# The down projection of an encoder block as one level of Strassen, with the activations' combinations kept in DRAM

## The chip, the cores and the metric

The kernel runs on one core of one Trainium2 chip. The metric is the device time of one execution in microseconds (us); lower is better. Three runs of the kernel before took 2248.24, 2250.68 and 2250.88 us, so its median is 2250.68 us.

## The reference, cut to what matters

```python
D_MODEL = 2048; SEQ = 512
D_FF = 5632                       # 44 tiles of 128 features
x = x + jnp.concatenate([ya, yb], axis=-1) @ w_out[l]     # after two groups of attention heads
h = rmsnorm(x, norm_ffn[l])
x = x + (jax.nn.silu(h @ w_gate[l]) * (h @ w_up[l])) @ w_down[l]
return rmsnorm(x, norm_final)
```

Everything is float32. The change concerns the feed-forward part: gate and up (2048 to 5632 each), their gated product, and the down projection (5632 to 2048).

## The kernel before, in words

**Precision.** Each float32 operand is split into a rounded high part and the rest, a low part, both of type fp32r. A product is three matmuls, high x high, high x low and low x high (`mm3`, lines 187 to 190). So every weight tile is loaded by DMA (SP's queue), cast to its high part by ScalarE (`act.copy`) and subtracted to its low part by VectorE (`dve.tensor_sub`).

**Order.** TensorE's instructions keep the order in which the program writes them (line 49). Those of the other engines and the DMAs are placed by a scheduler: program order is their priority, and an instruction may come forward when its data and its buffer are there.

**Stages.** Input projection with attention; output projection (`unit_out`); gate/up (`unit_gu`, 44 units, one for each feature tile); down projection (`unit_dn`, then `unit_last`).

**Gate/up** already works as one level of Strassen (the Winograd form with seven products). The 2 x 2 blocks are: up and gate on one side, halves of a pair of model tiles on the other, and the two halves of the 512 positions. `turn_x` (line 523) makes, for each of the eight pairs of model tiles, the seven combinations of the normalized input, 128 x 7 x 512 (high and low), and they stay on chip in the tiles `cp0` to `cp5`, `w0` and `w1`. For each unit `load_gu` (line 569) loads four blocks of weights, 512 KB each, three into the ring of places m0 to m5 and one into a staging buffer `st`; `make_gu` (line 580) adds them up on VectorE and splits each of the seven operands into high and low. The products run in the order of line 563; `made_gu` (line 604) keeps three products ahead, in five pairs of buffers. Each product is 8 pairs x 3 = 24 matmuls of 256 columns, and a unit 168. Four PSUM banks take the seven products: `al` takes 11 and 12, `be` s2, `gm` s3 and 22, `de` s1 and s4 (line 615). Between products, `after` (line 630) adds them up. At the end of the unit VectorE and ScalarE make the gated product (lines 670 to 673), and its 128 x 512 tile goes to DRAM (`acts_kept`).

**Down.** `act_tile` (line 677) loads a tile from `acts_kept` and splits it; 28 such tiles stay on chip. `unit_dn` (line 697) runs twice (20 tiles each) over four groups of 512 output columns. For each it accumulates four banks, one for each 128 positions: 20 x 4 x 3 = 240 matmuls of 512 columns. The activations are the stationary operand, the weights move. `batch` and `fetch` (lines 114 to 136) load and split the weights, one batch of two tiles ahead. `to_rest` adds the scaled result to the residual, which `load_rest` has put on chip. `unit_last` does the last four feature tiles, position tile by position tile and group by group, with the final normalization (`finish`) behind each.

```python
    for p in range(2):
        for g in range(4):
            drive(unit_dn(p, g))
    load_gfin()
    drive(unit_last())
```

Of the kernel before, what the change touches and what calls it, by code (L numbers as in the profile page):

```python
# [17 lines left out]
P = 128  # L18
# [10 lines left out]
HC = (NCH - 1) // 2  # L29
NP = KT // 2  # L30
LAST_OUT = 4 * 8 + 2 * H * 6 - 1
# [13 lines left out]
def encoder_block(ctx: ExitStack, tc: tile.TileContext, io):  # L45
# [40 lines left out]
    def y_tile():  # L86
        return pools["ys"].tile([P, 512], F32, name="y")

    def c_tile():
        return pools["acts"].tile([P, 1024], F32R, name="ac")  # L90
# [15 lines left out]
    for p in range(2):  # L106
        for g in range(4):
            order += [io["w4"][c, g, b] for c in range(p * HC, (p + 1) * HC) for b in range(2)]
    order += [io["w4"][NCH - 1, g, b] for g in range(4) for b in range(2)]
# [4 lines left out]
    def fetch():  # L114
        i = len(ready)
        st = wst.tile([P, 1024], F32, name="st")
        if i >= len(order) - 8:
            hi, lo = c_tile(), c_tile()
# [11 lines left out]
    def batch():  # L130
        i = state["next"]
        state["next"] += 1
        last = LAST_OUT if i <= LAST_OUT else len(order) - 1
        while len(ready) <= min(i + (AHEAD if i else 0), last):
            fetch()
        return ready[i]
# [319 lines left out]
    def unit_out(c):  # L456
        xr = []
        b = [bank() for _ in range(NT)]
        for kb in range(8):
            wh, wl = batch()  # L460
            if c == 3 and kb == 4:
                load_gu(0)
            if c == 3 and kb == 7:
                for n in PRODUCTS[:2]:
                    make_gu(0, n)
# [22 lines left out]
        if c == 3:  # L488
            for n in PRODUCTS[2:4]:
                make_gu(0, n)  # L490
        for t in range(NT):
            y = y_tile()
# [69 lines left out]
    acts = {}  # L562
    PRODUCTS = ("11", "s2", "s3", "s1", "12", "22", "s4")
    OPERAND = {"11": 0, "12": 1, "s4": 2, "s1": 3, "s2": 4, "s3": 5, "22": 6}
    made, raws, ring = [], {}, [0]

    at = [0]

    def load_gu(f):
        w = {}  # L570
        for j, n in enumerate(("11", "22", "21", "12")):
            if n == "21":
                w[n] = wst.tile([P, 1024], F32, name="st")
            else:
                w[n] = place(at[0] % 6)
                at[0] += 1
            nc.sync.dma_start(w[n], io["w3"][f, j])
        raws[f] = w

    def make_gu(f, n):  # L580
        if n == "11":
            if f + 1 < NF:
                load_gu(f + 1)
        w = raws[f]
        if n == "s2":
            w["s3"] = wst.tile([P, 1024], F32, name="st")
            dve.tensor_add(w["s3"], w["11"], w["21"])
            w["s1"] = w["21"]
# [3 lines left out]
        elif n == "s4":  # L592
            w["s4"] = w["s2"]
            dve.tensor_add(w["s4"], w["s2"], w["12"])
        i = ring[0]
        ring[0] += 1
        j = i % 5
        hi = place(6 + j, F32R) if j < 2 else wsh.tile([P, 1024], F32R, name="hi")
        lo = place(8 + j, F32R) if j < 2 else wsl.tile([P, 1024], F32R, name="lo")
        act.copy(hi, w[n])  # L600
        dve.tensor_sub(lo, w[n], hi.bitcast(F32))  # L601
        made.append((hi, lo))

    def made_gu(f, i):
        while len(made) <= min(f * 7 + i + (3 if f or i else 0), NF * 7 - 1):
            make_gu(*divmod_gu(len(made)))
        return made[f * 7 + i]

    def divmod_gu(j):
        return j // 7, PRODUCTS[j % 7]  # L610

    def unit_gu(f):

        al, be, gm, de = bank(), bank(), bank(), bank()
        into = {"11": al, "s2": be, "s3": gm, "s1": de, "12": al, "22": gm, "s4": de}
        s = slice(0, 256)
        u2, g = w_tile(), w_tile()
        t = w_tile()

        def product(i, pairs):  # L620
            n = PRODUCTS[i]
            wh, wl = made_gu(f, i)
            o = into[n][:, s]
            for p in pairs:
                x = x1t[p][:, OPERAND[n]]
                ws = slice(p * P, (p + 1) * P)
                mm3(o, wh[:, ws], wl[:, ws], x[:, :256], x[:, 256:], start=p == 0 and i < 4,
                    stop=p == NP - 1, skip_group_check=True)

        def after(i):  # L630
            if i == 0:
                act.copy(u2[:, s], al[:, s])
            elif i == 1:
                dve.tensor_add(u2[:, s], be[:, s], u2[:, s])
            elif i == 2:
                dve.tensor_add(t[:, s], gm[:, s], u2[:, s])
            elif i == 3:
                dve.tensor_add(g[:, 256:], de[:, s], t[:, s])
            elif i == 5:
                dve.tensor_add(g[:, s], gm[:, s], u2[:, s])  # L640
            elif i == 6:
                dve.tensor_add(t[:, 256:], de[:, s], u2[:, s])

        if f == 0:
# [8 lines left out]
            for i in range(4):  # L653
                product(i, range(6, 8))
                after(i)
                yield
        else:
            for i in range(4):
                product(i, range(8))
                after(i)  # L660
                yield
        for i in range(4, 7):
            product(i, range(8))
            after(i)
            if f == NF - 1 and i == 4:
                for n in range(2):
                    act_tile(n)
                    fetch()
            yield
        dve.tensor_mul(g, g, pools["rb2"])  # L670
        act.activation(g, g, AF.Silu, scale=-1.0)
        dve.tensor_mul(g[:, s], al[:, s], g[:, s])
        dve.tensor_mul(g[:, 256:], g[:, 256:], t[:, 256:])
        nc.sync.dma_start(acts_kept[f], g)


    def act_tile(f):
        if f not in acts:
            src = y_tile()
            nc.sync.dma_start(src, acts_kept[f])  # L680
            a = pools["mk"].tile([P, 1024], F32R, name=("raw", "sums")[f]) if f < 2 else c_tile()
# [5 lines left out]
    def load_rest():  # L687
        for t in range(NT):
            for c in range(4):
                y = pools["rest"].tile([P, 512], F32, name=f"rest{t}{c}")  # L690
                nc.sync.dma_start(y, x1_kept[t, c])
                rest[t, c] = y
# [3 lines left out]

    def unit_dn(p, g):
        b = [bank() for _ in range(NT)]
        fs = range(p * HC * CF, (p + 1) * HC * CF)
        for f in fs:  # L700
            if f % 2 == 0:
                w = batch()
            if g == 0:
                act_tile(min(f + 1, fs[-1]))
            elif g == 3:
                act_tile(min(fs[-1] + 1 + (f - fs[0]) // 5, NF - 1))
            a = act_tile(f)
            ws = slice((f % 2) * 512, (f % 2 + 1) * 512)
            for t in range(NT):
                mm3(b[t], a[:, t * P:(t + 1) * P], a[:, 512 + t * P:512 + (t + 1) * P],  # L710
                    w[0][:, ws], w[1][:, ws], start=f == fs[0], stop=f == fs[-1])
            yield
        for t in range(NT):
            to_rest(t, g, b[t])

    def unit_last():
        w = [batch() for _ in range(8)]
        for t in range(NT):
            for g in range(4):
                b = bank()  # L720
                for f in range(CF):
                    a, (wh, wl) = act_tile((NCH - 1) * CF + f), w[g * 2 + f // 2]
# [3 lines left out]
                yield  # L726
                to_rest(t, g, b)
# [4 lines left out]
    def load_gfin():  # L732
        for j in range(2):
            t = c_tile().bitcast(F32)
# [79 lines left out]
    for n in ("mx", "xa"):  # L814
        pools[n].release()
    pools["acts"] = stage("acts", 28)
    pools["rest"] = stage("rest", 1, "right")
    load_rest()
    for p in range(2):
        for g in range(4):  # L820
            drive(unit_dn(p, g))
    load_gfin()
# [69 lines left out]
```

## Time and profile before

| | |
|---|---|
| median of three runs | 2250.68 us |
| profiled execution | 2248.8 us, span 2246.6 us |
| TensorE clock granted, mean | 0.997 |
| busy VectorE, ScalarE over the span | 64%, 39% |
| DMA, mean | 115 GB/s; HBM read 236.41 MB, written 19.92 MB |
| gate/up | about 879 to 1758 us of the span |
| down projection | about 1758 to 2236 us, of which `unit_last` about the last 43 |

How to read it: PE is TensorE, PEld its weight loads, DVE is VectorE, ACT is ScalarE, POOL is GpSimd, SP issues DMAs. The page of the profile gives each engine's busy time, the chain of work that ended last, and groups of instructions by line with the mean time of one. Matmuls overlap each other, so the mean of one matmul (283 ns for 256 columns) is not what it costs; the number of them in a stretch of 100 us says that. The table of windows gives, for each stretch: its length, then busy time and count of each engine, the clock granted to TensorE (1.00 is full), the busy share of the 16 DMA engines, and GB/s.

### The profile page before, as it was taken

Reading aid. Unit: us, or ns where it says so; the run is one execution under the profiler, and the core shown is the slowest. Engines: PE = TensorE matmul, PEld = TensorE weight load, DVE = VectorE, ACT = ScalarE, POOL = GpSimd, SP = SyncE. Lnnn points to the kernel's source line nnn. Section 1 sums busy time; section 2 is a strip of 40 time slices with the busy share of each in tenths; the row PEclk is TensorE's granted clock in tenths of the full one; section 3 lists DMA queues with packets and bytes.
Section 4 is the critical chain, followed back from the end, with each engine's and each line's share of the span. In section 5 each row is a group of like instructions: output and inputs, shape, how many; then the busy total and the mean of one; then the engine's idle time right before and its main releaser. Section 6 shows DMA issues by size and latency. Waiting matters only on the chain.

```text
span 2246.6 us, 34376 instructions
## 1 busy us (share of the span) xinstructions
PE 2229.2 (99%) x14386; PEld 2032.8 (90%) x14386; DVE 1432.2 (64%) x2066; ACT 879.6 (39%) x1229; POOL 0.2 (0%) x4
## 2 busy tenths in 40 slices
PE   9999999999999999999999999999999999999998
PEld 8888888888888888999999999999999888888886
DVE  5655555677686348878888788878887532422236
ACT  6333333454564344444444344443444421311223
POOL 0000000000000000000000000000000000000000
PEclk9999999999999999999999999999999999999999
DMA  8222222222223452444433443334442743433342
GB/s 300 84 77 77 82 76 76 76 75 75 75 66 105 149 187 89 128 132 132 120 111 119 118 127 119 111 120 118 127 117 90 252 138 101 137 94 100 98 150 75
DMA packets 82714, 258.54 MB, mean 115 GB/s; under 512 B 9568, under 2 KB 9952, under 8 KB 82560
## 3 DMA queue, kind: packets, MB, share of 16 engines
q1 hardware_dynamic: 80256, 252.17, 35.8%
q10 hardware_dynamic: 2304, 4.20, 0.5%
q8 instruction: 112, 1.84, 0.3%
q14 instruction: 42, 0.34, 0.0%
HBM read 236.41 MB, written 19.92 MB: 114 GB/s over the span
## 4 chain that ended last, share of the span: by engine, by line
PE 98%; DVE 1%; ACT 0%; DMA 0%; issue 0%; SPq 0%; ACTq 0%
PE bank L189 32%; PE bank L190 32%; PE bank L188 32%; PE bank L307 1%; PE bank L407 1%; PE bank L408 1%; PE bank L535 0%; PE bank L432 0%; DMA st<-w 0%; PE bank L184 0%; DVE lo L125 0%; DVE w L546 0%; DVE sm L409 0%; DVE at L414 0%; ACT at L410 0%
## 5 line engine op out<-in xcount | busy, mean ns | idle before, releaser
L125 DVE TENSOR_TENSOR lo<-st,hi 128x1024 fp32r<-128x1024 f32 (+1 forms) x209 | 254.5, 1218 | 404.6 <-ACT hi L124 400.9
L124 ACT CAST hi<-st 128x1024 fp32r<-128x1024 f32 (+1 forms) x209 | 218.9, 1047 | 488.8 <-PE bank L190 356.0
L189 PE MATMUL bank<-cp,hi 128*128 128x256 f32 x1104 | 312.8, 283 | 0.0
L190 PE MATMUL bank<-cp,lo 128*128 128x256 f32 x1104 | 312.2, 283 | 0.0
L188 PE MATMUL bank<-cp,hi 128*128 128x256 f32 x1104 | 310.2, 281 | 0.0
L189 PE MATMUL bank<-lo,ac 128*128 128x512 f32 x608 | 236.6, 389 | 0.0
L188 PE MATMUL bank<-hi,ac 128*128 128x512 f32 x608 | 236.6, 389 | 0.0
L190 PE MATMUL bank<-hi,ac 128*128 128x512 f32 x608 | 236.5, 389 | 0.0
L600 ACT CAST hi<-m 128x1024 fp32r<-128x1024 f32 x130 | 136.4, 1049 | 226.0 <-PE bank L189 153.3
L189 PE MATMUL bank<-cp,m 128*128 128x256 f32 x744 | 210.5, 283 | 0.0
L188 PEld LDWEIGHTS bank<-cp,hi 128*128 128x128 f32 x1104 | 210.3, 191 | 0.0
L190 PE MATMUL bank<-cp,m 128*128 128x256 f32 x744 | 210.2, 282 | 0.0
L188 PE MATMUL bank<-cp,m 128*128 128x256 f32 x744 | 208.7, 280 | 0.0
L189 PEld LDWEIGHTS bank<-cp,hi 128*128 128x128 f32 x1104 | 207.8, 188 | 0.0
L190 PEld LDWEIGHTS bank<-cp,lo 128*128 128x128 f32 x1104 | 207.7, 188 | 0.0
L188 PE MATMUL bank<-xt,hi 128*128 128x512 f32 x512 | 205.9, 402 | 0.0
L190 PE MATMUL bank<-xt,lo 128*128 128x512 f32 x512 | 200.6, 392 | 0.0
L189 PE MATMUL bank<-xt,hi 128*128 128x512 f32 x512 | 200.0, 391 | 0.0
L601 DVE TENSOR_TENSOR lo<-m,hi 128x1024 fp32r<-128x1024 f32 x130 | 159.0, 1223 | 51.5 <-ACT hi L600 50.1
L600 ACT CAST m<-m 128x1024 fp32r<-128x1024 f32 x90 | 94.4, 1049 | 152.1 <-PE bank L189 104.2
L189 PE MATMUL bank<-lo,xt 128*128 128x256 f32 x512 | 145.0, 283 | 0.5 <-DVE lo L125 0.5
L188 PE MATMUL bank<-hi,xt 128*128 128x256 f32 x512 | 144.9, 283 | 0.1
(216 smaller groups left out, 4965.4 us busy)
## 6 DMA issues: line engine op xcount, KB each, us to landing
st<-w SPq DMA_DIRECT2D x259, 512.0 KB, 3.5
m<-w SPq DMA_DIRECT2D x132, 512.0 KB, 4.1
acts_kept<-wk SPq DMA_DIRECT2D x44, 256.0 KB, 4.3
y<-acts_kept SPq DMA_DIRECT2D x44, 256.0 KB, 4.3
at<-x SPq DMA_DIRECT2D x8, 512.0 KB, 8.9
wk<-x SPq DMA_DIRECT2D x16, 256.0 KB, 5.4
x_kept<-y ACTq DMA_DIRECT2D x16, 256.0 KB, 4.5
rest<-x_kept SPq DMA_DIRECT2D x16, 256.0 KB, 5.4
```

The source lines that it names most:

```text
L124: act.copy(hi[:, s], st[:, s])
L125: dve.tensor_sub(lo[:, s], st[:, s], hi[:, s].bitcast(F32))
L188: pe.matmul(out, lh, rh, start=start, stop=False, **kw)
L189: pe.matmul(out, lh, rl, start=False, stop=False, **kw)
L190: pe.matmul(out, ll, rh, start=False, stop=stop, **kw)
L307: pe.transpose(b[:, j * P:(j + 1) * P], prob[:, j * P:(j + 1) * P], ident)
L407: pe.matmul(b, q[:, qs], kh[:, cs], start=True, stop=False)
L408: pe.matmul(b, q[:, qs], kl[:, cs], start=False, stop=True)
L600: act.copy(hi, w[n])
L601: dve.tensor_sub(lo, w[n], hi.bitcast(F32))
```

## The change

**Down.** Pair 0 of feature tiles is done in the old way by `unit_first` (four groups, 96 matmuls of 512 columns), the last two pairs by `unit_last` as before. The 19 pairs between go through `unit_dn(c, u)` in five chunks of pairs (4, 4, 4, 4, 3) and four groups u of 512 output columns. One such unit is a Strassen level with seven products: each is pairs x 2 tiles of positions x 3 matmuls of 256 columns, with the combinations of activations as the stationary operand. The weights come as four blocks of 256 columns for each pair (`w5`, 512 KB a block for four pairs) and pass through the same `make` as gate/up's, now with four pairs of buffers instead of five. The results are added on chip into `acc` tiles; after the last chunk `add_x1` loads the residual and adds it.

**Combinations.** After each second gate/up unit `keep_combos` makes the seven combinations of the pair's activations, splits them (four tiles through three buffers) and stores them in DRAM, 128 x 7 x 512 float32, 1.84 MB for a pair. `load_operands` loads them again through GpSimd's queue into seven slots, the tiles that held gate/up's operands: chunk 0 at the start of `unit_first`, later ones three pairs during the second unit of the chunk before and a fourth at the chunk's start, where the first four products run over the three early pairs first.

**Gate/up.** The order of the products is new, and except in the first unit one bank `al` takes 11, s2, s1 and s4 one on the other; running sums are copied out by ScalarE after the first three products. The load of the next unit's weights stands at product 12 instead of 11.

**The end.** The weights and activations of `unit_last` use slots of `xa` and the common buffers, and are prepared in the last down unit and in `unit_last` (`prepare_last`, `last_pair`), no longer spread over the second half of the down projection.

```diff
+CHUNKS = [range(1 + 4 * c, min(5 + 4 * c, 20)) for c in range(5)]
+DN = 4
...
-        pools["ys"] = stage("ys", 5, "right")
+        pools["ys"] = stage("ys", 3, "right")
...
-    PRODUCTS = ("11", "s2", "s3", "s1", "12", "22", "s4")
+    PRODUCTS = ("11", "s3", "s2", "12", "s1", "22", "s4")
...
+    def make(i, name):
...
+        elif name == "12" and i + 1 < len(UNITS) and (i + 1) * 7 < limit[0]:
+            load_unit(i + 1)
...
+        if i < NF - 1:
+            j = j % 5 if j % 5 < 2 else None
+        else:
+            j = None if j % 4 else 0
+        hi = wsh.tile([P, 1024], F32R, name="hi") if j is None else place(6 + j, F32R)
+        lo = wsl.tile([P, 1024], F32R, name="lo") if j is None else place(8 + j, F32R)
+        act.copy(hi[:, :n], w[name])
+        dve.tensor_sub(lo[:, :n], w[name], hi[:, :n].bitcast(F32))
...
     def unit_gu(f):
-        al, be, gm, de = bank(), bank(), bank(), bank()
-        into = {"11": al, "s2": be, "s3": gm, "s1": de, "12": al, "22": gm, "s4": de}
+        apart = f == 0
+        al, be, gm = bank(), bank(), bank()
+        de = bank() if apart else al
+        into = {"11": al, "s3": gm, "s2": de, "12": be, "s1": de, "22": gm, "s4": de}
...
         def after(i):
             if i == 0:
-                act.copy(u2[:, s], al[:, s])
+                act.copy(s1, al[:, first])
             elif i == 1:
-                dve.tensor_add(u2[:, s], be[:, s], u2[:, s])
+                act.copy(q7, gm[:, first])
...
             elif i == 2:
-                dve.tensor_add(t[:, s], gm[:, s], u2[:, s])
+                act.copy(u2, al[:, first])
             elif i == 3:
-                dve.tensor_add(g[:, 256:], de[:, s], t[:, s])
+                dve.tensor_add(c11, be[:, first], s1)
+            elif i == 4:
+                dve.tensor_add(g[:, second], de[:, first], q7)
             elif i == 5:
-                dve.tensor_add(g[:, s], gm[:, s], u2[:, s])
-            elif i == 6:
-                dve.tensor_add(t[:, 256:], de[:, s], u2[:, s])
+                dve.tensor_add(g[:, first], gm[:, first], u2)
+                dve.tensor_mul(g, g, pools["rb2"])
+                act.activation(g, g, AF.Silu, scale=-1.0)
+                dve.tensor_mul(out[0], c11, g[:, first])
...
+    def keep_combos(i, raw):
+        sums = pools["mk"].tile([P, 1024], F32, name="sums").rearrange("p (a q) -> p a q", a=4)
+        dve.tensor_sub(sums[:, 0::2], raw[:, 1::2], raw[:, 0:1].to_broadcast([P, 2, 256]))
+        dve.scalar_tensor_tensor(sums[:, 1], sums[:, 0], -1.0, raw[:, 3], op0=OP.mult, op1=OP.subtract)
+        dve.scalar_tensor_tensor(sums[:, 3], sums[:, 1], -1.0, raw[:, 2], op0=OP.mult, op1=OP.subtract)
+        for o, src in ((0, raw[:, 1:3]), (2, raw[:, 3:4]), (3, sums[:, 0:2]), (5, sums[:, 2:4])):
+            n = src.shape[1]
+            y = y_tile(F32R).rearrange("p (n q) -> p n q", n=2)[:, :n]
+            split(y, src)
+            nc.sync.dma_start(combos[i][:, o:o + n], y.bitcast(F32))
...
+    def load_operands(c, some=slice(None)):
+        for i in CHUNKS[c][some]:
+            n = (i - 1) % 7
+            t = (pools["xa"], f"cp{n}") if n < 6 else (pools["mx"], "w0")
+            ops[i] = t[0].tile([P, 7, 512], F32R, name=t[1])
+            pool.dma_start(ops[i].bitcast(F32), combos[i])
...
+    def unit_dn(c, u):
+        pairs = CHUNKS[c]
+        apart = c > 0 and u == 0
+        if u == 0 and c > 0:
+            load_operands(c, slice(3, None))
+        if u == 1 and c + 1 < len(CHUNKS):
+            load_operands(c + 1, slice(0, 3))
...
+        def product(i, some):
+            n = PRODUCTS[i]
+            wh, wl = product_of(i0, i, 3 - i if some is early else 3)
+            for p in some:
+                x = ops[p][:, OPERAND[n]]
+                ws = slice((p - pairs[0]) * 256, (p - pairs[0] + 1) * 256)
+                for t in range(2):
+                    mm3(into[n][:, t * 256:(t + 1) * 256], x[:, t * P:(t + 1) * P],
+                        x[:, 256 + t * P:256 + (t + 1) * P], wh[:, ws], wl[:, ws],
...
+        def after(i):
+            if i == 0:
+                act.copy(s1, al)
+            elif i == 1:
+                add(2, 2, gm)
...
+            elif i == 2:
+                act.copy(u2, al)
+            elif i == 3:
+                add(1, 1, be)
+                add(1, 1, s1)
+            elif i == 4:
+                add(2, 2, de)
+                add(2, 1, u2)
+            elif i == 5:
+                add(2, 1, gm)
+            else:
+                add(1, 2, de)
+
+        early = pairs[:3]
+        if apart:
+            for i in range(4):
+                product(i, early)
+                yield
+        for i in range(7):
+            product(i, pairs[3:] if apart and i < 4 else pairs)
+            after(i)
+            if i0 == len(UNITS) - 1 and i == 3:
+                prepare_last()
+            yield
+        if c == len(CHUNKS) - 1:
+            for t in range(2):
+                add_x1(t, u)
...
+    drive(unit_first())
+    for c in range(len(CHUNKS)):
+        for u in range(DN):
+            drive(unit_dn(c, u))
     drive(unit_last())
```

More of the change, by code (lines that the diff above doesn't have):

```diff
@@ L132, in batch @@
         state["next"] += 1
-        last = LAST_OUT if i <= LAST_OUT else len(order) - 1
+        last = next(n for n in (LAST_OUT, len(order) - 9, len(order) - 1) if i <= n)
         while len(ready) <= min(i + (AHEAD if i else 0), last):
@@ L652, in unit_gu @@
                 advance()
[L653 to L663, printed above, removed]
+        for i in range(7):
+            product(i, range(6, 8) if apart and i < 4 else range(8))
             after(i)
             if f == NF - 1 and i == 4:
-                for n in range(2):
-                    act_tile(n)
-                    fetch()
+                act_tile(0, place(7, F32R))
+                act_tile(1, place(9, F32R))
+                fetch()
@@ L669, in unit_gu @@
             yield
[L670 to L677, printed above, removed]
+        if f // 2 in CHUNKS_ALL:
+            if f % 2:
+                keep_combos(f // 2, raw)
+        else:
+            for h in range(2):
+                nc.sync.dma_start(acts_kept[f][:, h * 256:(h + 1) * 256], out[h])
```

244 lines of the change are left out of this document (153 added, 91 removed).

## The prediction

> **What bounds the kernel now.** I read the page first: busy shares, then the chain that ended last.
>
> ```profile
> span 2246.6 us, 34376 instructions
> ...
> PE 2229.2 (99%) x14386; PEld 2032.8 (90%) x14386; DVE 1432.2 (64%) x2066; ACT 879.6 (39%) x1229; POOL 0.2 (0%) x4
> ...
> PE 98%; DVE 1%; ACT 0%; DMA 0%; issue 0%; SPq 0%; ACTq 0%
> ```
>
> TensorE is busy for 99% of the span and makes 98% of the chain, so every matmul column taken away counts, if nothing else takes its place. The mean hides stages, so I asked for stretches of 100 us: one inside gate/up, two inside the down projection.
>
> ```profile
> core 0: us, PE busy (x) PEld busy (x) DVE busy (x) ACT busy (x) POOL busy (x), PEclk, DMA share, GB/s
> ...
> 1400.00:1500.00 100.00, 100.00 (x837) 100.00 (x836) 81.08 (x96) 41.31 (x45) 0.00 (x0) 1.00 0.39 117
> ...
> 1900.00:2000.00 100.00, 100.00 (x442) 82.67 (x441) 37.92 (x41) 27.07 (x33) 0.00 (x0) 1.00 0.38 119
> ...
> 2100.00:2200.00 100.00, 100.00 (x443) 82.81 (x442) 35.60 (x36) 25.48 (x27) 0.00 (x0) 1.00 0.37 117
> ```
>
> These rows carry the argument. Gate/up already is a Strassen level with 256-column matmuls: 837 in 100 us, 0.1195 us each, one unit of 168 in 20.1 us, with VectorE at 81%. The down projection runs 512-column matmuls: 442 in 100 us, 0.2262 us each, with VectorE at 38% and 36%. So it has slack on every engine but TensorE. The change turns that stage into one that looks like gate/up.
>
> **The saving.** A pair of feature tiles costs 2 x 4 x 4 x 3 = 96 matmuls of 512 columns before. After, it costs 7 products x 2 row tiles x 3 passes x 4 output groups = 168 of 256 columns. 19 pairs: 1824 x 0.2262 = 412.6 us become 3192 x 0.1195 = 381.4 us, **31.2 us less**. Seven eighths of the columns would be 51.6 us; the narrower matmul, 0.2390 us for two halves, gives 20 us of it back. The pair in `unit_first` and the two in `unit_last` keep their 512 columns and cost the same. The Trainium skill says the same against narrow work ("Perfetto Trace Analysis", section "Matmuls": larger matmuls are more efficient), and "TensorE: Matmul & The Clock Gate", section "Back-to-back issue gap", gives 262 and 518 cycles at 2.4 GHz. By those figures, an estimate, the saving would be 45 us. The rows above are slower for both widths, and the narrow one is measured in the very form that the change uses; so that case gets no chance of its own.
>
> **What the saving needs from VectorE and ScalarE.** Prices by form:
>
> ```profile
> L601 DVE TENSOR_TENSOR lo<-m,hi 128x1024 fp32r<-128x1024 f32 x130 | 159.0, 1223 | 51.5 <-ACT hi L600 50.1
> ...
> L600 ACT CAST hi<-m 128x1024 fp32r<-128x1024 f32 x130 | 136.4, 1049 | 226.0 <-PE bank L189 153.3 <-DVE m L591 68.6 <-issue 2.8
> ...
> L695 DVE SCALAR_TENSOR_TENSOR rest<-bank,r,rest 128x512 f32<-128x512 f32 x48 | 34.2, 749 | 10.1 <-PE bank L190 10.1
> ...
> L670 DVE TENSOR_TENSOR wk<-wk,rb 128x512 f32<-128x512 f32 x44 | 30.5, 692 | 1.4
> ...
> L682 ACT CAST ac<-y 128x512 fp32r<-128x512 f32 x42 | 25.3, 619 | 16.8 <-PE bank L190 8.6 <-DMA y<-acts_kept 7.9
> ...
> L634 DVE TENSOR_TENSOR wk<-bank,wk 128x256 f32<-128x256 f32 x44 | 18.7, 424 | 29.3 <-PE bank L190 28.6 <-issue 0.7
> ...
> L632 ACT COPY wk<-bank 128x256 f32<-128x256 f32 x44 | 16.1, 365 | 0.0
> ```
>
> A gate/up unit of before adds up to 11 x 1.22 (seven low parts, four sums) + 5 x 0.42 + 0.69 + 2 x 0.42 = 17.1 us on VectorE. The window says 81% of 20.1 = 16.3, so neighbouring instructions overlap and a sum is worth 0.955 of itself.
> - *Down unit of four pairs:* 13.4 + 7 additions of 512 at 0.70 = 18.3, times 0.955 = 17.5 of 20.1 us (87%). ScalarE: 7 x 1.05 + 2 copies of 512, about 8.6 us. Both fit, so I cost them at nothing; with VectorE as the bound a unit could never cost less than 17.5.
> - *Gate/up:* one 0.42 addition fewer per unit (ScalarE gets two more copies of 0.365), and per pair `keep_combos`: 0.69 + 2 x 0.42 + 3 x 0.69 + 0.42 = 4.0 us. Net 3.2 us per 40.2 us, x 0.955: from 81% to 89%. It still fits.
> - *Last chunk, three pairs:* TensorE 126 x 0.1195 = 15.1 us a unit. A 768-wide VectorE instruction takes 0.95:
>
> ```profile
> 869.54 0.95 DVE L546 TENSOR_TENSOR w<-raw,w 128x768 fp32r<-128x768 f32 x1
> ```
>
> So VectorE has 11 x 0.95 + 4.9 + 4 x 0.42 (`add_x1`) = 17.0, x 0.955 = 16.3 us: it is **over** TensorE by 1.2 us a unit, 4.8 in four units, and the three products made ahead absorb part. I take 2 us (0 to 6).
>
> **Sharing one bank.** `al` now takes 11, s2, s1 and s4 in turn, so a reader has one product, 24 x 0.1195 = 2.9 us, before TensorE writes again; `de` used to have two or more. The readers are ScalarE copies after products 0 and 2 and a VectorE addition after product 4. Behind a waiting ScalarE copy stand the casts of later products, and VectorE's low parts wait for those.
>
> ```profile
> 1001.32 0.42 DVE L636 TENSOR_TENSOR wk<-bank,wk 128x256 f32<-128x256 f32 x1 [0.63 <-PE bank L190]
> ...
> 1004.73 0.42 DVE L638 TENSOR_TENSOR wk<-bank,wk 128x256 f32<-128x256 f32 x1
> ...
> 1009.94 0.42 DVE L640 TENSOR_TENSOR wk<-bank,wk 128x256 f32<-128x256 f32 x1 [0.32 <-PE bank L190]
> ```
>
> Of the three, L636 and L640 waited for TensorE; L638 came 3.4 us after L636, half a microsecond more than one product. VectorE is up to date here. A cast (1.05) ahead of a copy makes 1.4 us of 2.9, and a 1.22 ahead of the addition makes 1.65. So that alone stalls little: 0 to 1 us for the stage, I take 0.5 (the far end is the second rival).
>
> **Weight loads.** `load_unit` moves from product 11 to product 12, so its four 512 KB loads stand three products later in SP's program, behind the combination stores of the pair before. But ScalarE, VectorE and SP do not run in program order:
>
> ```profile
> L682 ACT CAST raw<-y x1: 622/622/622, 903.1 to 903.1; 128x512 fp32r<-128x512 f32 x1
> ```
>
> This cast stands in the program at the end of gate/up and ran at its beginning, when its data was there. Loads go when a buffer is free; a unit of 20.1 us hides a landing of 3.5 us. I cost the move at 0; without that cover each unit's first load would show, up to 4 us.
>
> **Operands through DRAM.** 1.84 MB per pair, 34.9 MB out and in. The loads go by GpSimd's queue, which has nothing else to hold up (4 instructions in the page's first row); no transfer of its own is in the trace. Nearest rows:
>
> ```profile
> st<-w SPq DMA_DIRECT2D x259, 512.0 KB, 3.5
> ...
> acts_kept<-wk SPq DMA_DIRECT2D x44, 256.0 KB, 4.3
> ```
>
> ```profile
> 10.00:20.00 10.00, 10.00 (x86) 10.00 (x85) 9.55 (x13) 9.38 (x13) 0.00 (x0) 1.00 1.03 414
> ...
> 1760.00:1770.00 10.00, 10.00 (x46) 8.17 (x45) 4.25 (x6) 2.69 (x4) 0.00 (x0) 1.00 1.01 345
> ```
>
> A full DMA moves 345 to 414 GB/s; a single 512 KB load alone makes 150.
> - *First chunk.* The slots are gate/up's operands, free only in its last product. From then 7.3 MB of operands and about 3.5 MB of weights must land before TensorE reaches the fourth pair, 96 x 0.2262 + 2.2 = 23.9 us after gate/up, with 2 us of head start. 10.8 MB take 26 to 31 us: a stall of 0 to 6, and at 300 GB/s 10. I take 3.5. A long stall also costs clock: after the wait at 880 the chain's matmuls took 0.21 instead of 0.12 us for 4.5 us, about 2 us lost.
>
> ```profile
> 879.93 0.21 PE bank L190
> ...
> 884.68 0.12 PE bank L189
> ```
>
> - *Later chunks.* Only one pair (8, 12, 16) comes at the boundary; it has 72 x 0.1195 = 8.6 us plus 2 of the product before, and needs 1.84 MB at some 300 GB/s, 6 us and a landing. The Trainium skill ("DMA: Bandwidth & Descriptors", "Anatomy of one DMA — SWDGE (gpsimd) path") fits 2.0 us + bytes/436 GB/s for a GpSimd transfer: an estimate of 6.2 us; no run here shows it yet. But four products now hold all four hi/lo buffers (the ring went from five to four): product 4's cast starts when product 0's rest ends, 2.15 us before TensorE wants it, and cast and low part take 2.3, with copies and additions of four products coming together. About 1.2 us each: 3.6 us in all (0 to 9).
>
> **The end.** Eight weight casts and four activation casts for `unit_last` used to lie in a stage with VectorE at 36%. Now 8 x 1.22 + 4 x 0.69 = 12.5 us meet the last chunk, where VectorE is full, and three of the pairs of buffers need slots that its operands hold. `unit_last` wants the last weights after three groups, 8.1 us. I take 3 us (0 to 9). The tail itself stays:
>
> ```profile
> 2236.27 0.24 PE bank L190
> ...
> 2241.44 0.61 ACTq L880
> ```
>
> **Sum.** -31.2 + 2 + 0.5 + 3.5 + 3.6 + 3 = -18.6, say -18. The profiled execution took 2248.8 us (span 2246.6 and 2.2 around it), the median of three runs is 2250.7, 1.9 more. Forecast: 2248.8 - 18 = 2231 for that execution, **2232** for the median.
>
> **Rivals.**
> - *All of it.* Every wait hidden: -31, 2219.5. For it: all engines but TensorE have room in most units. Against it: the first chunk's 10.8 MB in 24 us. 0.15.
> - *Slower: the combination stores hold ScalarE.* Four split tiles go out per pair through three buffers, so the fourth split waits until the first store has landed: sums (1.5) and low part (0.7) ahead, landing 4.3, so 6.5 us after the pair's end. If that split is queued ahead of the copy of `al`, which TensorE needs 5.7 us after the unit began, copy and cast end at some 8.5 and TensorE waits up to 2.8 us: 19 times, 53 us, giving 2272. It decides from 1.0 us per pair (19 us eat the forecast gain). For: in-order queues, buffers of three. Against: the order is made by readiness, as the early cast showed. 0.10.
> - *Operands come slowly.* If GpSimd's transfers move like single 512 KB loads, 150 GB/s, the first chunk takes 49 us, a stall of 25, and each boundary 2 to 4: about 2248, no change. Against: they are 3.5 times as long, and four are in flight. 0.12.
> - *Forecast* (stalls of 5 to 22 us; 2224 to 2241): 0.63.
>
> About 0.2% (4.5 us) is what a measurement can tell. Slower gets 0.10, no change 0.07 of the slow operands' 0.12, the rest is faster: 0.83. The range runs from just under the full saving, 2217, to the no-change rival, 2250.
>
> **What would show it.** After gate/up a gap on TensorE waiting for an operand tile, some 3 us; small gaps at three boundaries waiting for VectorE's low parts; 20.1 us per down unit; VectorE near 87%, and full in the last chunk. Wrong: gaps every 40 us in gate/up, a gap over 10 us at its end, or down units longer than 21 us.

## The result and the profile after

| | before | after |
|---|---|---|
| median of the runs beside each other, us | 2249.72 (four, 2248.24 to 2250.88) | 2226.30 (four, 2222.24 to 2229.36) |
| ratio to before, 95% interval | 1 | 0.9895 (0.9877 to 0.9914) |
| profiled execution, us | 2248.8 | 2224.93 |
| its span, us | 2246.6 | 2223.2 |

The change makes the kernel 23.4 us faster; the forecast was 2232, 18 us faster. The size is nearly right. The parts are not: three of them are off by 8 to 11 us each, and one of these, a gain in gate/up, is one that the kernel before reaches too, with its old products and accumulators, when its tiles are moved by 32 bytes.

First the page of the kernel after: the span, and the busy time of each engine.

```profile
span 2223.2 us, 37891 instructions
...
PE 2187.6 (98%) x15754; PEld 2058.0 (93%) x15754; DVE 1661.5 (75%) x2373; ACT 1000.2 (45%) x1486; POOL 10.4 (0%) x23
```

TensorE still sets the time, but it now stands still at places: 36 us of the span are not busy, 17 before. The windows show where. Columns as in the prediction: stretch, its length, busy time and count for TensorE, its weight loads, VectorE, ScalarE, GpSimd, then granted clock, DMA share, GB/s.

```profile
1400.00:1500.00 100.00, 100.00 (x846) 100.00 (x844) 83.97 (x101) 47.99 (x64) 0.00 (x0) 1.00 0.48 157
...
1800.00:1840.00 40.00, 40.00 (x355) 40.00 (x355) 36.85 (x39) 17.49 (x19) 0.00 (x0) 1.00 0.35 110
1895.00:1935.00 40.00, 40.00 (x340) 40.00 (x339) 35.91 (x38) 16.64 (x18) 0.46 (x1) 1.00 0.35 106
...
2100.00:2150.00 50.00, 50.00 (x426) 50.00 (x426) 49.15 (x71) 22.99 (x31) 0.00 (x0) 1.00 0.40 127
2150.00:2180.00 30.00, 24.78 (x144) 19.70 (x143) 26.38 (x41) 12.93 (x17) 0.00 (x0) 1.00 0.64 211
```

Gate/up makes 846 matmuls in 100 us, 837 before. The down part has two paces at full clock: 355 matmuls in 40 us in chunk 0, 340 in chunk 1. From 2100 to 2150 VectorE is busy for 98% of the time, and in the next 30 us TensorE loses 5. TensorE's waits from 1750 to 2165 (engine, tile and line of the waiting instruction, what it waited for; total, times, longest):

```profile
PE bank L184 <- DVE wk L810: 8.5, 3, 2.8
PE bank L185 <- DVE lo L613: 2.8, 1, 2.8
```

And from 2100 to 2200:

```profile
PE bank L185 <- DVE cp L121: 3.1, 4, 0.8
PE bank L185 <- DVE lo L121: 1.4, 2, 1.3
```

L613 and L121 make low parts of weights, L810 is the addition to `u2` at a chunk's boundary. All of TensorE's waits in these two stretches, but one of 0.6 us for a cast of ScalarE, end with VectorE, and none with an operand tile. TensorE is idle for 2.8 us in the longest; from the start of one matmul to the start of the next that is 3.1 us, and a gap is given in this way below unless it is called a wait.

To add this up I cut the trace into stages, from the start of a stage's first matmul to that of the next, counting matmuls (168 in a unit, 126 in the last chunk). The mean interval between the starts of two matmuls of a stage, without gaps and slow clock, is its pace. A stage is over its pace by what it took beyond its number of matmuls times that interval, and the rows on waits give this.

| term, us | forecast | measured in the profiled executions |
|---|---|---|
| columns of 19 pairs | -31.2 | -42.5 (1,824 x 0.2271 = 414.2; now 371.7) |
| pace of gate/up | 0 | -8.1 |
| waits in gate/up (shared bank) | +0.5 | +1.0 |
| first chunk | +3.5 | +3.3 |
| later chunks | +3.6 | +13.3 (12.3 at the boundaries 1 to 3, 1.0 behind one) |
| last chunk | +2 | 0.0 |
| end (`unit_last` 43.5, now 51.9) | +3 | +8.4 |
| start and tail | 0 | +1.2 |
| sum | -18.6 | -23.4 (span) |

### The profile page after: what moved, and what is told of

The parts are those of the page before. It is cut to its first block, busy times and chain, and to the rows that moved or that the text cites. A ratio compares the mean times of both kernels' runs of the same rounds, so it can differ in the third digit from the quotient of the medians.

```text
span 2223.2 us, 37891 instructions
## 1 busy us (share of the span) xinstructions
PE 2187.6 (98%) x15754; PEld 2058.0 (93%) x15754; DVE 1661.5 (75%) x2373; ACT 1000.2 (45%) x1486; POOL 10.4 (0%) x23
## 5 line engine op out<-in xcount | busy, mean ns | idle before, releaser
L612 ACT CAST hi<-m 128x1024 fp32r<-128x1024 f32 (+1 forms) x208 | 215.1, 1038 | 251.4 <-PE bank L185 124.4
L613 DVE TENSOR_TENSOR lo<-m,hi 128x1024 fp32r<-128x1024 f32 (+1 forms) x208 | 249.5, 1201 | 60.4 <-ACT hi L612 60.2
L121 DVE TENSOR_TENSOR lo<-st,hi 128x1024 fp32r<-128x1024 f32 (+1 forms) x136 | 165.0, 1214 | 142.6 <-ACT hi L120 138.9
L120 ACT CAST hi<-st 128x1024 fp32r<-128x1024 f32 (+1 forms) x136 | 141.7, 1042 | 194.9 <-PE bank L185 75.3
L185 PE MATMUL bank<-lo,cp 128*128 128x256 f32 (+1 forms) x738 | 209.0, 283 | 4.3 <-DVE lo L613 2.8
L184 PE MATMUL bank<-hi,cp 128*128 128x256 f32 (+1 forms) x738 | 208.8, 283 | 0.7 <-DVE sums L790 0.7
L186 PE MATMUL bank<-hi,cp 128*128 128x256 f32 (+1 forms) x738 | 208.8, 283 | 0.0
L184 PE MATMUL bank<-cp,m 128*128 128x256 f32 x732 | 205.4, 281 | 0.0
L185 PE MATMUL bank<-cp,m 128*128 128x256 f32 x732 | 204.2, 279 | 0.0
L186 PE MATMUL bank<-cp,m 128*128 128x256 f32 x732 | 204.2, 279 | 0.0
L612 ACT CAST m<-m 128x1024 fp32r<-128x1024 f32 (+1 forms) x112 | 116.8, 1043 | 144.2 <-PE bank L185 87.9
L613 DVE TENSOR_TENSOR m<-m,m 128x1024 fp32r<-128x1024 f32 (+1 forms) x112 | 135.3, 1208 | 39.1 <-ACT m L612 38.8
```

Of the source, the lines that this page charges most:

```text
L120: act.copy(hi[:, s], st[:, s])
L121: dve.tensor_sub(lo[:, s], st[:, s], hi[:, s].bitcast(F32))
L184: pe.matmul(out, lh, rh, start=start, stop=False, **kw)
L185: pe.matmul(out, lh, rl, start=False, stop=False, **kw)
L186: pe.matmul(out, ll, rh, start=False, stop=stop, **kw)
L612: act.copy(hi[:, :n], w[name])
```

## The experiments

Times below are of single profiled executions unless an interval is given; before took 2248.6 to 2249.3 beside them (medians where there were several). "The whole" is the time of the whole kernel. Single runs of one kernel differ by up to 7 us (after: 2222 to 2229), so each verdict rests on a stage, not on the whole.

**Where gate/up's 7.1 us come from.** The new constant `nr2` takes 32 bytes of SBUF as the program is laid out (a trace shows no addresses), and all tiles allocated behind it lie 32 bytes further on: `hi`, `lo`, the m tiles, `w0` and `w1`. The tiles `cp0` to `cp5` are allocated from the other end of SBUF, and a constant doesn't move them. So the first run gives the kernel before an unused constant and nothing else, the second gives the kernel after one more.

```diff
     acts = {}
+    pad = const.tile([P, NT], F32, name="pad")
+    dve.memset(pad, 0.0)
```

> The kernel of before with one unused 32-byte constant ahead of the tiles hi, lo, m0 to m9, w0 and w1, so that they lie 32 bytes further on, 32 past a multiple of 64 as in the kernel after; nothing else is changed. Theory (where the tiles lie makes the 7.1 us that gate/up gained): units 1 to 43 of gate/up go from 864.9 to about 857.7 us, the whole from 2249.7 to about 2243. Rival (the new order of the products and the shared bank make them): gate/up stays within 1 us of 864.9.

> The kernel after with one more unused 32-byte constant, so that hi, lo, the m tiles, w0 and w1 lie on multiples of 64 bytes as they did before. Theory of the place: units 1 to 43 of gate/up go from 857.7 to about 865 us, the whole from 2226.3 to about 2234. Rival (order and bank): gate/up stays within 1 us of 857.7.

The same stretch of 700 us of gate/up, in before, then in before with the pad, then in after, then in after with the pad:

```profile
1000.00:1700.00 700.00, 700.00 (x5849) 700.00 (x5848) 568.86 (x663) 287.30 (x313) 0.00 (x0) 1.00 0.40 119
```

```profile
1000.00:1700.00 700.00, 700.00 (x5904) 700.00 (x5903) 573.08 (x667) 290.36 (x316) 0.00 (x0) 1.00 0.41 121
```

```profile
1000.00:1700.00 700.00, 699.95 (x5897) 699.44 (x5896) 593.35 (x716) 338.47 (x455) 0.00 (x0) 1.00 0.47 154
```

```profile
1000.00:1700.00 700.00, 699.71 (x5913) 698.20 (x5912) 594.24 (x718) 339.59 (x457) 0.00 (x0) 1.00 0.46 154
```

The pad alone takes units 1 to 43 of the old gate/up from 864.9 to 856.8 us, and the whole to 2242.0; none of the 22 runs of before on record took less than 2247.4. That is all of the gain, and more: the kernel after takes 857.7, of which 1.0 us are waits. That it is the same gain in both can be read from the intervals between matmuls, averaged by the operand tile that they read (`cp0` to `cp5`, then `w0`, `w1`). In before they are 119.4, 120.8, 119.2, 120.8, 119.2, 120.8, 117.5 and 120.0 ns; with the pad 119.2, five times 117.8, 123.3 and 117.5; in the kernel after the same as with the pad, within 0.2 ns. The gain lies on the `cp` tiles, which the pad does not move, so the place of the weights that are read beside them has to do with it.

The second half of my theory fell: with 32 bytes more, back on multiples of 64, gate/up does not go back to 865 but takes 855.6 (the whole 2224.1). So the place of the tiles matters, and which rule of the place it follows isn't known. Against the padded kernel before, the change itself gains about 16 us (2242.0 in one run against 2226.3).

**The two paces of the down part.** In the kernel after, TensorE fell from 113.3 to 118.3 ns at the first matmul on operand tile `w0` in chunks 1 and 3, and went back only behind a stall. `w0` lies among the weights, the `cp` tiles above them.

```diff
-                x = x1t[p][:, OPERAND[n]]
+                x = x1t[p % 6][:, OPERAND[n]]
```

> The kernel after, whose gate/up products read the tiles of feature pairs 0 and 1 a second time in place of those of pairs 6 and 7 (tiles w0 and w1, which lie at the low addresses beside the weights), with as many matmuls as before: it leaves the last two pairs out of gate and up. In the down part TensorE changed from 113.3 to 118.3 ns a matmul each time at the first matmul on w0, and back only behind a stall. Theory (a tile of the low region read beside weights of the low region brings the slower pace, which then lasts): units 1 to 43 of gate/up go to 113.3 ns x 7224 = 818 us, 39 us less. Rival (the pace of gate/up is its own, and only the matmuls on w0 and w1 themselves, 120 ns, come down): 117.5 to 118.3 ns x 7224 = 849 to 855 us.

```diff
+        pools["two"] = stage("two", 1, "right")
+        pools["xa"] = stage("xa", 1, "right")
...
-            t = (pools["xa"], f"cp{n}") if n < 6 else (pools["mx"], "w0")
-            ops[i] = t[0].tile([P, 7, 512], F32R, name=t[1])
+            ops[i] = pools["xa"].tile([P, 7, 512], F32R, name=f"cp{n}")
```

> The kernel after with all seven operand tiles of the down part at the upper addresses (cp0 to cp6) and six of the eight result tiles in w0 and w1 in their place. Theory (low region): the 1,848 matmuls of chunks 1, 3 and 4 go from 118.3 to 113.3 ns, 9.2 us less in all. Rival (GpSimd's bursts of four loads at the chunk boundaries bring the slower pace): chunks 1, 3 and 4 stay at 118.3 ns, and the whole within 1.5 us of 2226.

Without `w0` and `w1` gate/up took 852.9 us, 117.8 ns a matmul: the rival's number, not 818 (the whole 2219.7). With seven `cp` tiles the chunks changed places:

```profile
1800.00:1840.00 40.00, 40.00 (x342) 40.00 (x341) 36.16 (x38) 17.10 (x19) 0.00 (x0) 1.00 0.34 106
1895.00:1935.00 40.00, 40.00 (x355) 40.00 (x355) 36.44 (x39) 17.43 (x19) 0.00 (x0) 1.00 0.36 110
```

Now chunk 0 is slow and chunk 1 fast, the whole unchanged at 2225.3. My theory fell, and bursts of loads don't explain it either, since they came at the same places. Over all runs chunk 1 was fast as a whole only here, without `w0`; chunks 0 and 2 were fast in some runs and slow in others, chunk 3 never fast as a whole. Each change of pace I looked at came at `w0` or at an interruption of the stream of matmuls, be it one interval of 0.24 us, as at 1792 in the kernel after, or of 0.63, as at 1793 here (one of 0.19, at 1990.6 in the kernel with paced loads below, went with a change too). What an interruption leads to isn't predictable from what I saw, so what sets the pace stays open. It moves a chunk of four units by 3 us, and so the whole by some microseconds from kernel to kernel.

**The boundaries.** In the kernel after, the gap at the first boundary reads thus on VectorE (start, duration, what it did, idle time before):

```profile
1862.64 0.69 DVE L790 TENSOR_TENSOR y<-wk,y 128x512 f32<-128x512 f32 x1 [5.42 <-ACT wk L806]
1863.25 0.68 DVE L790 TENSOR_TENSOR y<-bank,y 128x512 f32<-128x512 f32 x1
1863.85 1.21 DVE L613 TENSOR_TENSOR m<-st,m 128x1024 fp32r<-128x1024 f32 x1
1864.98 1.22 DVE L613 TENSOR_TENSOR lo<-m,hi 128x1024 fp32r<-128x1024 f32 x1
1866.12 0.68 DVE L810 TENSOR_TENSOR wk<-bank,wk 128x512 f32<-128x512 f32 x1
```

While four products run over their early pairs, VectorE has nothing to do for 5.4 us: no product is complete and no hi/lo buffer is free. Then everything comes at once, and TensorE, which wants the bank of s2 for s1, waits for the fifth in the row (L810). Two causes are possible, so each was taken away by itself.

```diff
+        fe = bank() if apart else al
-        into = {"11": al, "s3": gm, "s2": de, "12": be, "s1": de, "22": gm, "s4": de}
+        into = {"11": al, "s3": gm, "s2": de, "12": be, "s1": fe, "22": gm, "s4": fe}
...
-                add(2, 2, s1)
-                add(1, 2, s1)
+                add(2, 2, u2)
+                add(1, 2, u2)
```

> The kernel after with a fifth bank in the first unit of chunks 1 to 4: the products of s1 and s4 are summed in a bank of their own, and u2 is added where the first product's copy was, as many additions as before. In the kernel after TensorE's gap of 3.1 us at each of the boundaries 1 to 3 ends with the addition that reads the bank of s2 (2166.8 less 300: 1866.8), while the low part of the weights for s1 was there at 1865.1. Theory 1 (the shared bank makes the gap): each of the three gaps shrinks from 3.1 to about 1.3 us, the three first units lose 5 to 7 us of their 12.3 over the normal pace, the whole goes to about 2220. Rival (the ring of four hi/lo buffers, which holds back the next low part until the first product is through): the gap then ends with the low part instead and is still 2 us or more.

(The bracket there should read 1866.8 alone.)

```diff
-        if i < NF - 1:
+        if i < NF - 1 or i > NF:
             j = j % 5 if j % 5 < 2 else None
```

> The kernel after with five hi/lo buffers in place of four from the second Strassen unit on (m7 and m9, which held the two plain activation tiles until then). Theory 2 (the ring of four): VectorE's idle 5.4 us ahead of 1862.6 take the low part of s1, the addition to u2 comes about 2.3 us sooner, and each of the three boundary gaps shrinks from 3.1 to 0.8 us or less, with no half clock behind it: 8 to 11 us less, the whole about 2216 to 2218. Rival (the shared bank): the gaps stay above 2 us.

TensorE's waits with the fifth bank, then with five buffers:

```profile
PE bank L185 <- DVE m L613: 3.5, 3, 1.2
PE bank L184 <- DVE y L791: 2.6, 4, 0.9
```

```profile
PE bank L184 <- DVE wk L810: 5.1, 3, 1.7
```

Both are causes, in series. With the bank the three gaps are 1.4 us and end with the low part of s1, as expected, but a gap of 1.0 to 1.2 us comes 6.5 us later: the boundaries are 7.3 us over their pace, not 12.3. With the buffers the gaps are 2.0 us, not 0.8, and still end with L810; 5.9 us over. Neither made the whole faster (2227.3, 2225.8): with the fifth bank the last two Strassen units lost 4.2 us, with the five buffers the first one 4.5 more, where TensorE waited for a late copy of ScalarE. (That wait, at 1777, comes before the first product that uses the new buffers; the weight block whose addition ScalarE waited for ahead of the copy landed at 1777.4, as late as in the kernel after, see below.)

**The first chunk.** GpSimd's queue was empty, so at the end of gate/up it issued chunk 0's four loads and chunk 1's first three at once. The next run ties the three to units 1, 2 and 3.

```diff
-        if u == 1 and c + 1 < len(CHUNKS):
-            load_operands(c + 1, slice(0, 3))
...
                 act.copy(s1, al)
+                if u and c + 1 < len(CHUNKS):
+                    load_operands(c + 1, slice(u - 1, u), s1)
...
+            if behind is not None:
+                pool.tensor_copy(ops[i][:, 0, :1], behind[:, :1])
             pool.dma_start(ops[i].bitcast(F32), combos[i])
```

> The kernel after, whose three early operand loads of the next chunk wait for units 1, 2 and 3 of the chunk, one each (GpSimd writes one column of the new tile from the copy of that unit's first product, and then issues), in place of all three being issued at once. Theory (seven loads of 1.84 MB in a burst at the end of gate/up hold the 128 KB store of the last activations for 19 us, so ScalarE and VectorE come late): the store lands within 12 us, TensorE's 3.1 us at 1781 go, the first unit takes 19.9 us or less in place of 23.0, the whole is 3 us less. Rival (the work of ScalarE and VectorE there is too much whatever the transfers do): the gap stays over 2 us. At the later boundaries nothing changes by either.

The gap went: the first unit took 20.2 us instead of 23.0, 0.9 over its pace instead of 3.3, the whole 2220.0. But not by the way I gave: the last store landed 19.4 us after its issue with seven loads and 19.6 with four, and ScalarE waited 6.8 us in both. The difference is in VectorE's queue, in after and then in the paced kernel:

```profile
1777.62 1.23 DVE L593 TENSOR_TENSOR st<-m,st 128x1024 f32<-128x1024 f32 x1 [9.78 <-issue]
1778.88 1.22 DVE L596 TENSOR_TENSOR st<-st,m 128x1024 f32<-128x1024 f32 x1
1780.02 1.22 DVE L613 TENSOR_TENSOR lo<-m,hi 128x1024 fp32r<-128x1024 f32 x1
```

```profile
1773.64 1.23 DVE L593 TENSOR_TENSOR st<-m,st 128x1024 f32<-128x1024 f32 x1 [6.65 <-issue]
```

L593 adds two weight blocks of the next unit. Its block `st` was issued at 1766.73 and landed at 1777.54, 10.8 us, with the DMA full; in the paced kernel 7.7 us. The low part that TensorE needs is queued behind that addition. In the four runs with paced loads the first unit was 0.1 to 1.4 us over its pace, in the eight others of the change 2.5 to 7.8.

**The end.** ScalarE's casts of the last eight weight tiles waited for loads that come one by one through the staging ring of three (waits from 2140 to 2185):

```profile
ACT cp L120 <- DMA st<-w: 7.1, 4, 2.2
...
ACT hi L120 <- DMA st<-w: 3.0, 3, 1.7
```

```diff
         if i >= len(order) - 8:
+            st = place(at[0] % 6)
+            at[0] += 1
             hi, lo = last_pair(i - len(order) + 8)
```

> The kernel after, whose last eight weight tiles are loaded through the six tiles m0 to m5 instead of the staging ring of three that the last unit's other loads use. The last unit takes 51.9 us, 43.5 of them at full pace. Theory 1 (the ring of three holds the loads back, 2 us from one to the next): 43.5 to 45 us, the whole 7 to 8 us less. Theory 2 (VectorE is full: of 2100 to 2180 it is idle for some 5 us only): at most 4 to 5 us less, and the rest of the gaps is then VectorE work without idle time ahead of it.

```diff
             for t in range(2):
-                add_x1(t, u)
+                rest[t, u] = acc[u, t // 2][:, (t % 2) * 512:(t % 2 + 1) * 512]
```

> The kernel with the last weights loaded through m0 to m5, without the residual addition of the last chunk (8 loads of x1 and 16 additions of VectorE, 0.40 us each, 6.4 us): it leaves x1 and the scale r2 out of token blocks 0 and 1. With the loads alone moved, the last unit ran at full pace but the last Strassen unit lost 4.1 us ahead of it. Theory (VectorE's work is the limit at the end, the loads only its form): the last Strassen unit goes back to 14.8 us and the last unit stays at 43.5 to 44, 4 us less than with the loads alone, 2216. Rival (the bank that the last unit's first product waits for, or the loads, hold it whatever VectorE has to do): 2 us or more of the 4.1 stay.

With the loads moved, the last unit runs at full pace (44.1 us), but the last Strassen unit takes 18.9 us instead of 14.8: TensorE waits 2.5 us for an addition, and then runs slow. The two together go from 66.7 to 63.0 (the whole 2220.0). Without the residual addition, and so without its eight loads, they take 59.1, and 58.4 is full pace. The window from 2150 to 2180 in this kernel:

```profile
2150.00:2180.00 30.00, 30.00 (x197) 27.30 (x196) 29.75 (x46) 14.96 (x23) 0.00 (x0) 1.00 0.46 149
```

So the end's 8.4 us are two causes as well, some 4 us each: the staging ring, and VectorE's work behind it. (The loads of x1 went with the additions; but with the weight loads moved and x1 still added, VectorE is idle for only 0.4 us between 2138 and 2160, which speaks for its work.) (The whole took 2222.9, since chunk 0 ran at 118 here and two boundaries cost 5.8 each.)

**Relief by other engines, and all together.** In the next two kernels ScalarE scales the residual rows of the last chunk in place and GpSimd adds x1.

```diff
+                act.activation(y[:, s], y[:, s], AF.Copy, scale=r[:, t:t + 1])
...
+            pool.tensor_add(y, y, x1)
```

> Paced operand loads, the last weights through m0 to m5, and the residual addition of the last chunk by ScalarE (the scale, in place) and GpSimd (the sum) instead of VectorE. If the three costs are separate: 4.5 us from the first chunk and what follows it, 7.7 from the end, the whole 2213 to 2215. Rival (GpSimd's additions are slow or keep VectorE from its memory): the last Strassen unit keeps its 4 us, the whole 2216 to 2218.

> All of that, and the fifth bank and the five hi/lo buffers at the boundaries together. Theory 1 (each was one half of the boundary's 3.1 us: with the bank alone the gap was 1.4 us and ended with the low part of s1, with the buffers alone 2.0 us and ended with the addition to u2): the gaps go, the three first units come within 1 us of their pace, 10 us less than without them, the whole 2203 to 2206. Rival (VectorE's additions only come later: 1.0 to 1.5 us gaps in the unit after each boundary, as both single runs had at places): 2208 to 2212.

GpSimd is no relief. Its additions, then VectorE at the same time:

```profile
2116.81 3.36 POOL L856 TENSOR_TENSOR y<-y,wk 128x512 f32<-128x512 f32 x2 [29.63 <-ACT y L852]
...
2150.44 4.03 POOL L856 TENSOR_TENSOR raw<-raw,wk 128x512 f32<-128x512 f32 x2 [14.79 <-ACT raw L852]
```

```profile
2149.53 0.68 DVE L730 TENSOR_TENSOR cp<-st,cp 128x512 fp32r<-128x512 f32 x1
2150.13 1.22 DVE L123 TENSOR_TENSOR cp<-m,cp 128x1024 fp32r<-128x1024 f32 x1
2151.26 2.06 DVE L615 TENSOR_TENSOR lo<-m,hi 128x768 fp32r<-128x768 f32 x1
```

One addition takes 1.7 to 2.0 us there, 0.7 on VectorE, and a low part of 0.95 us took 2.06 beside it. The Trainium skill speaks of both: "GPSIMD Engine Reference", section "4.1 Engine selection", puts GpSimd at about half VectorE's speed for operations with two inputs, and "SBUF — State Buffer", section "Who interferes with whom", says that a VectorE instruction with two SBUF inputs contends with a GpSimd instruction that reads SBUF. The rows agree with the second, and show GpSimd slower than the first says: 2.4 to 2.9 times VectorE's time, with both engines at work. The last two Strassen units lost 4.7 us, and the whole was 2224.3 (0.9881, 0.9867 to 0.9896): the rival's gap, at a slower pace than it reckoned with, all chunks at 118. With bank and buffers together the gaps at the boundaries are 1.3 us and the three units 3.7 us over their pace instead of 12.3, as neither did alone. The end lost 7.1 us and the tail 3, so it took 2218.7 (0.9868, 0.9851 to 0.9884), above both ranges that were expected.

The last kernel leaves GpSimd's additions out, and has the fifth bank only where a fourth pair comes late (chunks 1 to 3) and the five buffers from chunk 1 on.

> Paced operand loads, the last weights through m0 to m5 with the residual addition left on VectorE, the fifth bank at the boundaries of chunks 1 to 3 alone, five hi/lo buffers from chunk 1 on. By the single runs: first chunk and what follows 3 to 4 us less than in the kernel after, the three boundaries 12.3 us over their pace down to 3.7, 8.6 less (as with bank and buffers together), the end 3.7 less (8 less in the last unit, 4 more ahead of it): about 2226.3 - 16 = 2210. Rival (the whole moves with the pace of 113 or 118 ns that each chunk falls into, which no edit here chooses): 2215 to 2219, with the stages' excess over their own pace as low as said, and the normal pace of two or three chunks 118 in place of 113.

```profile
PE bank L186 <- DVE y L794: 3.4, 4, 1.0
PE bank L186 <- DVE w L794: 2.1, 1, 2.1
```

It takes **2208.2 us** (five runs, 2207.7 to 2211.5), 0.9822 of before (0.9809 to 0.9836), 18 less than the change as it was. Over their pace: first unit 0.6, boundaries 3.8, end 3.3, the first two as expected, the end 1.4 better. The rival's slow pace was there too, in chunks 0, 1, 3 and 4, and cost 2.0 us against the kernel after.

## Why the forecast was nearly right

That the sum came near is luck in good part: the columns and gate/up gave 19.4 us more than forecast, the waits took 13.4 us more, start and tail 1.2.

- **Columns, -31.2, measured -42.5.** The mechanism was right, the price of a narrow matmul too high: 0.1164 us on the mean of the down part, not the 0.1195 of gate/up in before, which makes 9.7 of the 11.3 us; a unit of four pairs at its pace took 19.0 or 19.9 us, not 20.1. The other 1.6 us are the wide matmul's: counted from start to start it took 0.2271 us, not 0.2262, since a window also counts the matmuls that only reach into it. The row of gate/up carried the cost of where before's tiles lay, which the padded kernel showed, and knew nothing of the pace of 113 ns. The estimate by the Trainium skill's "TensorE: Matmul & The Clock Gate", section "Back-to-back issue gap", 45 us, that I set aside came nearer, though no row here reaches its 262 cycles (109 ns); the fastest is 113. The wide matmuls, at 227 ns, don't reach its 518 cycles (216 ns) either, and the two differences nearly cancel.
- **Engines.** VectorE needs 17.5 us for a unit of four pairs, as worked out (36.85 of 40 us, units of 19.04); the share is 92%, not 87%, since the unit is shorter. The last chunk did not run over: VectorE is 98% busy there, and what didn't fit went into the end.
- **Shared bank, +0.5, measured +1.0.** Right in size. The longer gaps stand ahead of product s1 in units with an even number, and at the longest, an interval of 0.33 us at 1083.7, the copy of `al` came late because ScalarE had waited 2.6 us for a store of the combinations: the shared bank and the second rival meet there. What gate/up gained came from a place that no part of my sum looked at: the addresses.
- **First chunk, +3.5, measured +3.3.** The size was right and the cause wrong. No operand was late: the fourth tile landed at 1773.0, and TensorE came to it about 2.2 us after 1772.5. I counted four loads, and as GpSimd's queue waits for nothing, seven went, and a weight block behind them was late.
- **Later chunks, +3.6, measured +13.3.** This step failed. I named the buffers and the additions that come together, and priced a gap at 1.2 us. I left out that the new order makes TensorE wait for the addition itself, for the bank, fifth in VectorE's row, that the gap is then 3.1 us, and that TensorE's clock falls behind two of the three:

```profile
1950.50:1953.50 3.00, 3.00 (x16) 3.00 (x17) 3.00 (x4) 0.00 (x0) 0.00 (x0) 0.55 0.98 416
```

  The operand itself was in time (1.84 MB, 7.9 us from issue to landing with the DMA to itself at first, against the 6.2 estimated).
- **End, +3, measured +8.4.** VectorE was named; the staging ring, which lets one load of 512 KB through in about 2 us, was not.
- **Rivals.** "All of it" did not come out: the time is 6.8 us above its 2219.5, and the waits were there, 26 us of them. The forecast's own 2224 to 2241 holds the time, but its stalls of 5 to 22 us don't hold the waits; columns and addresses, 19 us better than forecast, made up for them. Slow operands: the seven moved at 424 to 432 GB/s together between 1760 and 1780. The combination stores do hold ScalarE, 2.2 us for each of 19 pairs:

```profile
ACT y L626 <- DMA combos<-y: 41.7, 19, 2.6
```

  but TensorE lost 1.0 us by all waits of gate/up together, far below the 1.0 us a pair from which that rival decides.

## What to carry to other kernels

Before crediting a rearrangement with a gain, give the old kernel the new one's memory layout: here 32 unused bytes were worth 8 us. A queue that waits for nothing issues everything it can reach, so count what is ready at that moment, and tie prefetches to the progress of the work. Where work waits for a buffer and for a bank, lifting one shows little; look at who is idle before the gap, and lift both.

## What was not expected of the hardware

- Shifting SBUF tiles by 32 bytes changed the 256-column matmuls of the kernel before, at full clock, from 119.7 to 118.6 ns; in the kernel after, 32 bytes more took them from 118.6 to 118.1.
- The same matmuls at the same granted clock run at 113.3 or at 117.8 to 118.3 ns for whole chunks, and one interval of 0.24 us in the stream was enough to change between them. What chooses was not settled.
- A gap of 3.1 us cost another 1.5 us of slow clock in two of three cases in the kernel after (0.55 and 0.62 granted), and none in the third; gaps of 2.0 us and less at the same places cost none. A gap of 2.75 us ahead of the last unit, in the kernel with its weight loads moved, was followed by 2.6 us at 0.50.
- A store of 128 KB beside four or seven loads of 1.84 MB took 15 to 20 us to land, against 3.9 as the median of such stores.
